# Hybrid block on one core: a weight sum moved ahead in the convolution's projection, stores moved to another engine in the mixing, loads put on another queue at the MLP's seam

## The chip, the core and the metric

The kernel runs on one core of a Trainium2 chip. The metric is device microseconds of one execution; the time of a kernel is the median of its runs. Five engines work side by side, each through its own list of instructions in order: TensorE (PE; its weight loads are shown apart as PEld), VectorE (DVE), ScalarE (ACT), GpSimd (POOL) and SyncE (SP), the last of which only issues transfers here. A transfer is issued by an instruction of one of these engines into a queue and lands some microseconds later. An instruction that needs another's result, or a buffer that is still in use, waits, and everything behind it on its engine waits with it.

## The reference, cut to what matters

```python
SEQ, D_MODEL, CONV_WIDTH, ATTN_WIDTH, D_FF = 512, 2048, 1024, 1024, 8192

h = rmsnorm(x, g_mix)
z = h @ w_in
cb, cc, cv, q, k, v, f_logit, gate_c, gate_a = split(z)
conv_branch = (cb * causal_dwconv(cc * cv, conv_w)) @ w_conv_out
attn_branch = forgetting_attention(q, k, v, log_sigmoid(f_logit + b_f)) @ w_attn_out
merged = sigmoid(gate_c + b_gate_c) * conv_branch + sigmoid(gate_a + b_gate_a) * attn_branch
x = x + merged @ w_mix_out                 # the mixing
h = rmsnorm(x, g_mlp)
u = square(relu(h @ w_ff1))                # first MLP product
x = x + u @ w_ff2                          # second MLP product
return rmsnorm(x, g_final)
```

One batch, one layer, everything in float32.

## The kernel before, in words

All large products are float32 at float32's accuracy, made from a faster format: each operand is split into a high part (`th`, a rounding by ScalarE, line 111) and a low part (`tl`, the rest, a subtraction by VectorE, line 114), and TensorE adds three products: high by high, low by high (lines 171 and 175, or 195 and 197), and high by low (line 177, or 199).

On top of that, each product of two matrices is done by quarters with seven products in place of eight. They are named A11, A12, A22 (quarters as they are) and S1, S2, S3, S4 (sums of quarters). For each of the seven the weights' quarter or sum is made in place by `sub` (VectorE, line 128), split into `th` and `tl`, and multiplied with the matching sum of the activations. The accumulators are `a`, `b`, `c`, `d`; `snap` (ScalarE, line 268, `o<-a`) and `plus` (VectorE, line 131, `o<-c,o`) bring them out and combine them, and `put` takes the finished quarter. A `Group` is one such product for a block of columns: `head` does A11 and A12, and `tail`, `tail2` or `tail3` do the rest in different orders. Its weights are loaded by SyncE into four slots (`x0` to `x3`).

The order of instructions on each engine is set by a scheduler from the program's order, except where `keep_in_program_order` pins an instruction or `issue_after` ties it to another. Four stages matter here.

*Conv.* `conv_out(c, banks)` multiplies the convolution's output by `w_conv_out`, for c = 0 to 3, 512 columns each, with `Columns` groups and `tail2`. The weights' tiles are called `y`, and the stationary operand `ys`. Behind A12 the hook `group.after["A12"]` makes the first sum (`first_sum`, X00 <- X01 - X00, S1's operand). The sum for S3 (X01 <- X11 - X01) is made in `tail2`, behind the call that runs S1. Blocks 0 and 3 multiply their result by gates (`merged<-o,gates`, line 1235, for block 0) that are loaded into four tiles under the tag `hg`.

*Mixing.* Four groups g multiply `merged` by `w_mix_out`. While group g + 1 runs, `Mix` forms the seven operands of group g's result for the MLP. `Mix.out` writes five of them: it splits an operand into `staged` (high, ScalarE) and the operand itself (low, VectorE), and stores both in `h_d` with transfers issued by GpSimd (line 1416). There are fifteen such pairs, since group 3 keeps its parts on chip.

*First MLP product.* `ff1(g, ...)` makes 16 groups of columns of `h @ w_ff1`. The list `later` holds work put off from the group before: applying ReLU and square, forming sums (`r`, `rh`) of the result and storing them to `s_d` (lines 1464 to 1484). `tail` runs that list behind S2's `snap` and ahead of S3.

*Seam.* The second MLP product runs in units, `unit(seg, cg, ST)`, each with four 1 MB weight tiles `y` (line 1708), and with operands `us` that `load_sums` reads back from `s_d` (line 1607): `US[1]` holds those of S2 and S3, `US[2]` of S1 and A22, `US[3]` of S4. For the first unit, `US[1]` is loaded by GpSimd right behind the last group of the first product, and `US[2]` and `US[3]` by SyncE in the middle of the unit's code.

Of the kernel before, what the change touches and what calls it, by code (L numbers as in the profile page):

```python
# [8 lines left out]
F32 = mybir.dt.float32  # L9
# [6 lines left out]
P = 128  # L16
# [29 lines left out]
def tile_hybrid_block(ctx: ExitStack, tc, x, g_mix, w_in, b_f, b_gate, conv_w, w_conv_out,  # L46
# [168 lines left out]
    class Group:  # L215
# [3 lines left out]
        def __init__(self, view, c1, c2, w, ST, mm, banks, put, scale=1.0, extra={}, after=None, shift=SHIFT):  # L219
            self.extra, self.after, self.shift = extra, {} if after is None else after, shift  # L220
            self.view, self.cs, self.w, self.ST, self.mm, self.banks = view, (c1, c2), w, ST, mm, banks
            self.put, self.scale, self.at = put, scale, {}
            self.begun, self.queue, self.X = False, nc.sync, {}
            self.pinned, self.mid, self.apart, self.ready = False, {}, False, {}
            self.freed, self.summed, self.paced, self.half = lambda: None, False, False, {}
            self.nq = view.shape[0] // (2 * P)

        def load(self, i, j):
# [105 lines left out]
        def tail(self):  # L334

            X = self.quarters((0, 1), (1, 1))
            a = self.a
            c = self.acc("c")
            self.run(c, "S4", X[1, 1], True)
            sub(X[0, 0], X[0, 1], X[0, 0])  # L340
            sub(X[0, 1], X[1, 1], X[0, 1])
            sub(X[1, 1], X[1, 1], X[0, 0])
            self.run(a, "S2", X[1, 1], False)
            sub(X[1, 0], X[1, 0], X[1, 1])
            self.done(1, 1)
# [44 lines left out]
        def tail2(self):  # L390

            X = self.quarters((0, 1), (0, 0), (1, 1), (1, 0))
            a = self.a
            if not self.pinned:
                sub(X[0, 0], X[0, 1], X[0, 0])
            c = self.acc("c")
            self.run(c, "S1", X[0, 0], True)
            if not self.summed:
                third = sub(X[0, 1], X[1, 1], X[0, 1])
            if self.pinned and not self.summed:  # L400
                tc.keep_in_program_order(third)
# [744 lines left out]

    class Columns(Group):


        def load(self, i, j):  # L1150
            if (1 - i, j) not in self.at:
                self.at[i, j] = main.tile([P, 2, self.nq, self.w], F32, tag=f"x{slot()}", name=f"y{j}")
            else:
                self.at[i, j] = self.at[1 - i, j]
            t, c = self.at[i, j][:, i], self.cs[j]
# [57 lines left out]
    def conv_out(c, banks):  # L1213

        gates = {}
        if c in GATED:
            for i, j in ((0, 0), (1, 1), (0, 1), (1, 0)):
# [14 lines left out]
        def put(i, j, v):  # L1232
            ts = slice(i * HS, (i + 1) * HS)
            if c == 0:
                nc.vector.tensor_tensor(out=whole_of[c][:, i, :, j, :], in0=v, in1=gates[i, j], op=ALU.mult)
# [121 lines left out]
    class Mix:  # L1357
# [50 lines left out]
        def out(self, n, src):  # L1408
# [3 lines left out]
            else:  # L1412
                hi = staged()
                split_in_order(src, hi, src)
                for e, o in enumerate((hi.bitcast(F32), src)):
                    nc.gpsimd.dma_start(out=h_d[:, SPLIT.index(n), e, 2 * g:2 * g + 2], in_=o)

        def first_of(self):
            self.s1 = pm.tile([P, 2, HS], F32, tag="s1", name="s1")
# [181 lines left out]
    def load_sums(seg, ks, ST, queue=nc.gpsimd):  # L1601

        for k in ks:
            place, names = US[k]
            t = main.tile([P, 2, 4, len(names), HS], F32R, tag=f"t{place}", name="us")
            for e in range(2):
                queue.dma_start(out=t[:, e].bitcast(F32), in_=s_d[seg][:, e, :, 2 * k:2 * k + len(names)])
# [12 lines left out]
    later.pop()()  # L1620
    ph.close()
    pp.close()
# [70 lines left out]
    def unit(seg, cg, ST):  # L1693
# [9 lines left out]
        for i, j in ((0, 1), (1, 1), (0, 0), (1, 0)) if end else ((0, 0), (1, 0), (0, 1), (1, 1)):  # L1703
# [4 lines left out]
            nc.sync.dma_start(out=t, in_=src[i])  # L1708
            X[i, j] = t

        def run(ps, n, src, first):
            hi, lo = parts([P, 4, S])
            split(src, hi, lo)
            mm_rows(ps, ST[n], hi, lo, first)

        last = seg == NSEG - 1
        begun = set()
# [67 lines left out]
        into(1, 0, a)  # L1785
        run(d, "S3", X[0, 1], True)
        free.append(at[0, 1])
        into(1, 1, d)
        run(a, "S1", X[0, 0], False)
# [51 lines left out]
```

## Time and profile before

| | |
|---|---|
| time, median of 3 runs | 2413.63 us (2411.69 to 2413.76) |
| profiled execution | 2415.49 us |
| its span on the engines | 2413.4 us |
| TensorE busy | 2396.1 us (99%), 17778 matmuls |
| VectorE, ScalarE, GpSimd busy | 2029.7, 1205.2, 297.8 us |
| clock granted to TensorE | full speed (tenths of 9 in all 40 slices) |
| transferred | 491.98 MB, mean 204 GB/s |

How to read it: times in the trace are microseconds from the start of the span. A row of the timeline has its start, its duration, the engine, the line of the code, the operation, output and inputs, the shape, and in brackets the idle time ahead of it with what ended it. TensorE's matmuls overlap, so a matmul of 128x256 is listed with 0.28 us, while the next one starts 0.113 us later: gaps are read from start to start. TensorE idles for 17.3 us of the span in all.

### The profile page before, as it was taken

What the parts mean: (1) busy time and instruction counts of PE and PEld (TensorE: products, weight loads), DVE (VectorE), ACT (ScalarE), POOL (GpSimd) and SP (SyncE); (2) the same over time, 40 slices, a digit from 0 to 9 for tenths busy, and PEclk for the clock granted to TensorE, in tenths of its full rate; (3) what the DMA queues carried; (4) which work ended last, traced back from release to release, by engine and by line L of the source; (5) the groups of instructions that cost most, each with busy time, mean ns of one, the idle gap of its engine ahead of it and who ended that gap; (6) DMA issues with size and microseconds to landing.
All of it is one profiled execution on the core that took longest, in us unless ns stands there. A gap on an engine that the chain in (4) does not pass through costs nothing. (4 is left out here: it accounts for less than half of the span.)

```text
span 2413.4 us, 41364 instructions
## 1 busy us (share of the span) xinstructions
PE 2396.1 (99%) x17778; PEld 2259.7 (94%) x17778; DVE 2029.7 (84%) x1683; ACT 1205.2 (50%) x1238; POOL 297.8 (12%) x476
## 2 busy tenths in 40 slices
PE   9999999999999999999999999999999999999998
PEld 9999999999999999899999999999998888888886
DVE  7987677789888778889988889888887888889898
ACT  7443444445555534456666666665664333333334
POOL 1110111121111112023300000000011001100000
PEclk9999999999999999999999999999999999999999
DMA  8664544564565756566856564655678567665662
GB/s 276 190 189 152 156 147 152 154 205 158 172 209 175 262 180 209 165 211 223 311 195 217 194 231 172 222 207 197 231 294 293 165 209 253 218 211 184 233 230 102
DMA packets 281127, 491.98 MB, mean 204 GB/s; under 512 B 11820, under 2 KB 192136, under 8 KB 280560
## 3 DMA queue, kind: packets, MB, share of 16 engines
q1 hardware_dynamic: 228496, 275.86, 36.1%
q0 software_dynamic: 51840, 212.42, 24.0%
q8 instruction: 139, 2.28, 0.4%
q10 hardware_dynamic: 608, 1.06, 0.1%
q14 instruction: 44, 0.36, 0.0%
HBM read 379.70 MB, written 109.07 MB: 203 GB/s over the span
## 5 line engine op out<-in xcount | busy, mean ns | idle before, releaser
L111 ACT ACTIVATE th<-x 128x2048 fp32r<-128x2048 f32 (+1 forms) x280 | 537.1, 1918 | 487.9 <-DVE x L128 165.4
L114 DVE TENSOR_TENSOR tl<-x,th 128x2048 fp32r<-128x2048 f32 (+2 forms) x282 | 639.7, 2274 | 156.2 <-ACT th L111 152.4
L128 DVE TENSOR_TENSOR x<-x,x 128x2048 f32<-128x2048 f32 (+1 forms) x160 | 366.1, 2288 | 22.0 <-DMA x<-in_w_in_dram 16.9
L111 ACT ACTIVATE th<-y 128x2048 fp32r<-128x2048 f32 (+1 forms) x109 | 185.3, 1701 | 272.1 <-PE a L197 138.8
L114 DVE TENSOR_TENSOR tl<-y,th 128x2048 fp32r<-128x2048 f32 (+1 forms) x109 | 219.0, 2014 | 28.3 <-ACT th L111 27.8
L195 PE MATMUL a<-th,us 128*128 128x512 f32 x512 | 199.3, 389 | 0.0
L197 PE MATMUL a<-th,us 128*128 128x512 f32 x512 | 199.2, 389 | 0.0
L171 PE MATMUL c<-S,th 128*128 128x256 f32 x848 | 196.0, 277 | 0.0
L175 PE MATMUL c<-S,th 128*128 128x256 f32 x848 | 195.8, 277 | 0.0
L171 PE MATMUL a<-S,th 128*128 128x256 f32 x784 | 182.4, 278 | 0.2 <-ACT o L268 0.2
L175 PE MATMUL a<-S,th 128*128 128x256 f32 x784 | 180.8, 276 | 0.0
L171 PEld LDWEIGHTS c<-S,th 128*128 128x128 f32 x848 | 159.3, 188 | 0.1
L175 PEld LDWEIGHTS c<-S,th 128*128 128x128 f32 x848 | 159.3, 188 | 0.0
L171 PEld LDWEIGHTS a<-S,th 128*128 128x128 f32 x784 | 147.3, 188 | 0.9 <-issue 0.5
L175 PEld LDWEIGHTS a<-S,th 128*128 128x128 f32 x784 | 147.3, 188 | 0.5 <-issue 0.5
L199 PE MATMUL a<-tl,us 128*128 128x512 f32 x512 | 136.9, 389 | 0.6 <-DVE tl L114 0.6
L171 PE MATMUL b<-A,th 128*128 128x256 f32 x544 | 126.2, 278 | 1.4 <-ACT th L111 1.4
L171 PE MATMUL a<-A,th 128*128 128x256 f32 x544 | 126.8, 279 | 0.0
L171 PE MATMUL d<-S,th 128*128 128x256 f32 x544 | 126.3, 278 | 0.0
L171 PE MATMUL d<-A,th 128*128 128x256 f32 x544 | 125.8, 277 | 0.0
L175 PE MATMUL a<-A,th 128*128 128x256 f32 x544 | 125.7, 277 | 0.0
L175 PE MATMUL b<-A,th 128*128 128x256 f32 x544 | 125.6, 277 | 0.0
(407 smaller groups left out, 6028.4 us busy)
## 6 DMA issues: line engine op xcount, KB each, us to landing
x<-in_w_in_dram SPq DMA_DIRECT2D x86, 1024.0 KB, 6.0
y<-in_w_ff_dram SPq DMA_DIRECT2D x64, 1024.0 KB, 7.7
x<-in_w_ff_dram SPq DMA_DIRECT2D x60, 1024.0 KB, 8.2
us<-s_d POOLq DMA_DIRECT2D x46, 1024.0 KB, 9.5
s_d<-rh POOLq DMA_DIRECT2D x32, 896.0 KB, 5.7
s_d<-r POOLq DMA_DIRECT2D x32, 896.0 KB, 6.1
x<-in_w_mix_out_dram SPq DMA_DIRECT2D x17, 1024.0 KB, 6.8
g_d<-o POOLq DMA_DIRECT2D x32, 256.0 KB, 3.1
```

The source lines that it names most:

```text
L111: return tied(nc.scalar.activation(out=hi, in_=src, func=AF.Copy))
L114: return tied(nc.vector.tensor_tensor(out=lo, in0=src, in1=hi.bitcast(F32), op=ALU.subtract))
L128: return nc.vector.tensor_tensor(out=out, in0=a, in1=b, op=ALU.subtract)
L171: i = nc.tensor.matmul(o, hi[:, q, js], Sh, start=first and q == 0 and j == 0, stop=False, skip_group_check=True)
L175: nc.tensor.matmul(o, hi[:, q, js], Sl, start=False, stop=False, skip_group_check=True)
L195: tied(nc.tensor.matmul(o, Sh, hi[:, q, :], start=begin and q == 0, stop=False, skip_group_check=True))
L197: tied(nc.tensor.matmul(o, Sl, hi[:, q, :], start=False, stop=False, skip_group_check=True))
L199: tied(nc.tensor.matmul(o, Sh, lo[:, q, :], start=False, stop=q == nq - 1, skip_group_check=True))
```

## The change

There are five edits.

1. Conv: `two_sums` makes the sum for S3 right behind the first sum, pinned in that order, after A12; `tail2` leaves it out by the flag `third`. The four gates of a block become one tile, `four`, of one place, and for c = 2 the second weight tile uses that place and not a weight slot. The gated product of block 0's quarter (0, 0) is put on `later`, which `tail2` empties behind S3.
2. Mixing: ScalarE, and not GpSimd, issues the store of the high part in `Mix.out`, pinned in program order.
3. First MLP product, g = 1: with `late` the list `later` is run behind S3 and its `snap`, not ahead of S3.
4. Seam: `US[1]`, `US[2]` and `US[3]` are all loaded on SyncE's queue, right behind the four weight tiles of the first unit.
5. Seam: in the first unit the sum `sub(t2, X10, t2)` for S4 is issued behind the low part of S3.

```diff
+        def two_sums(self):
+            self.first_sum()
+            X = self.quarters((1, 1))
+            tc.keep_in_program_order(sub(X[0, 1], X[1, 1], X[0, 1]))
+            self.third = True
...
# tail
-            while later:
+            while later and not self.late:
                 later.pop(0)()
             d = self.acc("d")
             self.run(d, "S3", X[0, 1], True)
             self.done(0, 1)
             d1 = self.snap(d, self.scale)
+            while later:
+                later.pop(0)()
...
# tail2
-            if not self.summed:
+            if not self.summed and not self.third:
                 third = sub(X[0, 1], X[1, 1], X[0, 1])
...
# Columns.load
+                if self.beside and j == 1:
+                    self.at[i, j] = pc_.tile(shape, F32, tag="hg", name=f"y{j}")
+                else:
+                    self.at[i, j] = main.tile(shape, F32, tag=f"x{slot()}", name=f"y{j}")
...
# conv_out
-                gates[i, j] = pc_.tile([P, 2, HS], F32, tag="hg", name="gates", bufs=4)
+            four = pc_.tile([P, 4, 2, HS], F32, tag="hg", name="gates")
+                gates[i, j] = four[:, n]
...
+                if (i, j) == (0, 0):
+                    later.append(gated)
+                else:
+                    gated()
...
-        group.after["A12"], group.apart = group.first_sum, True
+        group.after["A12"], group.apart, group.beside = group.two_sums, True, c == 2
...
# Mix.out
-                for e, o in enumerate((hi.bitcast(F32), src)):
-                    nc.gpsimd.dma_start(out=h_d[:, SPLIT.index(n), e, 2 * g:2 * g + 2], in_=o)
+                tc.keep_in_program_order(
+                    nc.scalar.dma_start(out=h_d[:, SPLIT.index(n), 0, 2 * g:2 * g + 2], in_=hi.bitcast(F32)))
+                nc.gpsimd.dma_start(out=h_d[:, SPLIT.index(n), 1, 2 * g:2 * g + 2], in_=src)
...
# first MLP product
+        group.late = g == 1
...
-    load_sums(0, (1,), us0)
...
# unit
+        begins = seg == 0 and cg == 0
+        if begins:
+            load_sums(0, (1, 2, 3), us0, nc.sync)
...
-        if seg == 0 and cg == 0:
-            load_sums(0, (2, 3), us0, nc.sync)
...
-        sub(t2, X[1, 0], t2)
+        if not begins:
+            sub(t2, X[1, 0], t2)
+        into(1, 0, a)
+        low = run(d, "S3", X[0, 1], True)
+        if begins:
+            with tc.issue_after(low.ins):
+                sub(t2, X[1, 0], t2)
```

What this does to the order of instructions, at the places that matter. A number behind a name tells buffers apart, and `x2` means two in a row.

VectorE in the conv's block 0, between A12 and S3, before (`y_9254` holds the quarters X00 and X10, `y_9318` X01 and X11; so the first sum is `y_9254<-y_9318,y_9254`, and the sum for S3 `y_9318<-y_9318`):

```order
L114 TENSOR_TENSOR tl<-y_9254,th 128x1024
L128 TENSOR_TENSOR y_9254<-y_9318,y_9254 128x1024
L114 TENSOR_TENSOR tl<-y_9254,th 128x1024
L128 TENSOR_TENSOR y_9318<-y_9318 128x1024
L131 TENSOR_TENSOR o<-b,o 128x512
L128 TENSOR_TENSOR y_9254<-y_9318,y_9254 128x1024
L1235 TENSOR_TENSOR merged<-o,gates 128x2x256
L114 TENSOR_TENSOR tl<-y_9318,th 128x1024
L114 TENSOR_TENSOR tl<-y_9254,th 128x1024
```

And now:

```order
L114 TENSOR_TENSOR tl<-y_9251,th 128x1024
L128 TENSOR_TENSOR y_9251<-y_9315,y_9251 128x1024
L128 TENSOR_TENSOR y_9315<-y_9315 128x1024
L114 TENSOR_TENSOR tl<-y_9251,th 128x1024
L128 TENSOR_TENSOR y_9251<-y_9315,y_9251 128x1024
L131 TENSOR_TENSOR o<-b,o 128x512
L114 TENSOR_TENSOR tl<-y_9315,th 128x1024
L1252 TENSOR_TENSOR merged<-o,gates 128x2x256
```

The sum for S3 stands one `tl` earlier, and the gated product behind a `tl` that it stood ahead of.

ScalarE in the mixing, from the first `staged` of group 0's parts to the `th` of S3 in group 1, before:

```order
L111 ACTIVATE staged<-f 128x512
L111 ACTIVATE th<-x_11421 128x2048
L111 ACTIVATE staged<-f 128x512
L111 ACTIVATE staged<-s_11390 128x512
L268 ACTIVATE o<-d 128x512
L111 ACTIVATE staged<-f 128x512 x2
L111 ACTIVATE th<-x_11309 128x2048
```

And now:

```order
L111 ACTIVATE staged<-f 128x512
L1438 DMA h_d<-staged 128x512
L111 ACTIVATE th<-x_11415 128x2048
L111 ACTIVATE staged<-f 128x512
L269 ACTIVATE o<-d 128x512
L1438 DMA h_d<-staged 128x512
L111 ACTIVATE staged<-s_11384 128x512
L1438 DMA h_d<-staged 128x512
L111 ACTIVATE staged<-f 128x512
L1438 DMA h_d<-staged 128x512
L111 ACTIVATE th<-x_11303 128x2048
```

Four issues stand on ScalarE, and one `staged` of the five has moved behind that `th`. Elsewhere in this stage, in group 3, three matmuls of `c<-th` (S4), which stood ahead of eight `a<-tl`, stand some forty instructions later on TensorE.

ScalarE in the first MLP product, group 1, around S3, before:

```order
L1492 ACTIVATE o<-o,common 128x512
L1469 ACTIVATE r<-c 128x512
L1464 ACTIVATE r<-o 128x256
L1464 ACTIVATE c<-o 128x512
L111 ACTIVATE th<-x_13212 128x2048
L1480 ACTIVATE rh<-r 128x1792
L111 ACTIVATE th<-x_13210 128x2048
L268 ACTIVATE o<-a 128x512
```

And now:

```order
L1515 ACTIVATE o<-o,common 128x512
L1492 ACTIVATE r<-c 128x512
L111 ACTIVATE th<-x_13206 128x2048
L1487 ACTIVATE r<-o 128x256
L1487 ACTIVATE c<-o 128x512
L1503 ACTIVATE rh<-r 128x1792
L111 ACTIVATE th<-x_13204 128x2048
L269 ACTIVATE o<-a 128x512
```

Two operations moved behind the `th` of S3; `rh` and the `th` of S1 still precede `o<-a`.

VectorE in the first unit of the second MLP product, from S2's operand to S1's low part, before:

```order
L114 TENSOR_TENSOR tl<-t_19644,th 128x2048
L1481 TENSOR_TENSOR r<-r,rh 128x1792
L128 TENSOR_TENSOR t_19644<-y_19638,t_19644 128x2048
L114 TENSOR_TENSOR tl<-y_19640,th 128x2048
L114 TENSOR_TENSOR tl<-y_19636,th 128x2048
```

And now:

```order
L114 TENSOR_TENSOR tl<-t_19644,th 128x2048
L1504 TENSOR_TENSOR r<-r,rh 128x1792
L114 TENSOR_TENSOR tl<-y_19631,th 128x2048
L128 TENSOR_TENSOR t_19644<-y_19629,t_19644 128x2048
L114 TENSOR_TENSOR tl<-y_19627,th 128x2048
```

The low part of S3 stands ahead of the sum for S4. On SyncE's queue the `us` loads behind the four weights are six now, four before:

```order
L1733 DMA y_19627<-in_w_ff_dram 128x4x512
L1733 DMA y_19629<-in_w_ff_dram 128x4x512
L1733 DMA y_19631<-in_w_ff_dram 128x4x512
L1733 DMA y_19633<-in_w_ff_dram 128x4x512
L1630 DMA us<-s_d_80 128x4x512 x4
L1630 DMA us<-s_d_80 128x4x256 x2
```

GpSimd's two `us` loads behind the last group are gone.

More of the change, by code (lines that the diff above doesn't have):

```diff
@@ L225, in __init__ @@
             self.freed, self.summed, self.paced, self.half = lambda: None, False, False, {}
+            self.late, self.third = False, False
             self.nq = view.shape[0] // (2 * P)
@@ L397, in tail2 @@
             self.run(c, "S1", X[0, 0], True)
-            if not self.summed:
+            if not self.summed and not self.third:
                 third = sub(X[0, 1], X[1, 1], X[0, 1])
-            if self.pinned and not self.summed:
-                tc.keep_in_program_order(third)
+                if self.pinned:
+                    tc.keep_in_program_order(third)
             d = self.acc("d")
@@ L1147, in tile_hybrid_block @@
     class Columns(Group):
+        beside = False
         def load(self, i, j):
             if (1 - i, j) not in self.at:
-                self.at[i, j] = main.tile([P, 2, self.nq, self.w], F32, tag=f"x{slot()}", name=f"y{j}")
+                shape = [P, 2, self.nq, self.w]
+                if self.beside and j == 1:
+                    self.at[i, j] = pc_.tile(shape, F32, tag="hg", name=f"y{j}")
+                else:
+                    self.at[i, j] = main.tile(shape, F32, tag=f"x{slot()}", name=f"y{j}")
             else:
@@ L1216, in conv_out @@
         if c in GATED:
-            for i, j in ((0, 0), (1, 1), (0, 1), (1, 0)):
-                gates[i, j] = pc_.tile([P, 2, HS], F32, tag="hg", name="gates", bufs=4)
+            four = pc_.tile([P, 4, 2, HS], F32, tag="hg", name="gates")
+            for n, (i, j) in enumerate(((0, 0), (1, 1), (0, 1), (1, 0))):
+                gates[i, j] = four[:, n]
                 k = 4 * c + 2 * j
@@ L1234, in put, with gated @@
             if c == 0:
-                nc.vector.tensor_tensor(out=whole_of[c][:, i, :, j, :], in0=v, in1=gates[i, j], op=ALU.mult)
+                def gated():
+                    nc.vector.tensor_tensor(out=whole_of[c][:, i, :, j, :], in0=v, in1=gates[i, j], op=ALU.mult)
+                if (i, j) == (0, 0):
+                    later.append(gated)
+                else:
+                    gated()
             elif c > 1:
@@ L1606, in load_sums @@
             for e in range(2):
-                queue.dma_start(out=t[:, e].bitcast(F32), in_=s_d[seg][:, e, :, 2 * k:2 * k + len(names)])
+                i = queue.dma_start(out=t[:, e].bitcast(F32), in_=s_d[seg][:, e, :, 2 * k:2 * k + len(names)])
+                if queue is nc.sync:
+                    tc.keep_in_program_order(i)
             for e, n in enumerate(names):
@@ L1709, in unit @@
             X[i, j] = t
+        begins = seg == 0 and cg == 0
+        if begins:
+            load_sums(0, (1, 2, 3), us0, nc.sync)
         def run(ps, n, src, first):
             hi, lo = parts([P, 4, S])
-            split(src, hi, lo)
+            low = split(src, hi, lo)[1]
             mm_rows(ps, ST[n], hi, lo, first)
+            return low
         last = seg == NSEG - 1
@@ L1782, in unit @@
         sub(X[0, 1], X[1, 1], X[0, 1])
-        sub(t2, X[1, 0], t2)
+        if not begins:
[5 more added lines that the diff above has]
+                sub(t2, X[1, 0], t2)
         free.append(at[1, 0])
-        into(1, 0, a)
-        run(d, "S3", X[0, 1], True)
         free.append(at[0, 1])
```

## The prediction

> **What bounds the kernel.** I read the busy shares first, then TensorE's own waits (columns: total us, times, longest us).
>
> ```profile
> PE 2396.1 (99%) x17778; PEld 2259.7 (94%) x17778; DVE 2029.7 (84%) x1683; ACT 1205.2 (50%) x1238; POOL 297.8 (12%) x476
> ...
> PE d L195 <- ACT th L111: 1.1, 1, 1.1
> PE d L199 <- DVE tl L114: 0.8, 2, 0.6
> PE a L199 <- DVE tl L114: 0.6, 1, 0.6
> ```
>
> TensorE is busy for 2396.1 of the span's 2413.4 us, and the change takes no matmul away. So there are two things to win: the 17.3 us in which it stands, and the rate at which it runs. No wait here is much over 1 us. I therefore took the stages that the diff touches one by one: where TensorE stands there, what ends that, and whether the new order removes it. The 2.1 us of the profiled 2415.49 that lie outside the span stay.
>
> **Conv.** Three weight loads wait in this stage; the first of them I follow back.
>
> ```profile
> PEld d L164 <- ACT th L111: 0.4, 1, 0.4
> PEld d L177 <- DVE tl L114: 0.3, 1, 0.3
> PEld c L171 <- DVE o L131: 0.3, 1, 0.3
> ...
> 888.93 1.22 DVE L114 TENSOR_TENSOR tl<-y,th 128x1024 fp32r<-128x1024 f32 x1 [1.19 <-ACT th L111]
> 890.07 1.22 DVE L128 TENSOR_TENSOR y<-y 128x1024 f32<-128x1024 f32 x1
> 891.40 1.06 ACT L111 ACTIVATE th<-y 128x1024 fp32r<-128x1024 f32 x1 [2.51 <-PE c L175]
> 892.52 0.36 PE L164 MATMUL d<-ys,th 128*128 128x192 f32 x1 [0.21 <-ACT th L111]
> ```
>
> The sum `y<-y` of 890.07 makes the operand of S3. It stands behind a `tl` ahead of which VectorE idled 1.19 us, waiting for the `th`. The change puts the 1.22 us sum into this hole: the `tl` comes 0.03 later, the sum more than 1 us earlier. S3's `th` is then bound by the place that TensorE frees (`PE c`, row 891.40). The sum ended at 891.29, just before that `th` began, so I can't tell which of the two was last; the 0.4 goes wholly or not at all, and I take wholly, since the sum is the operand itself. In block 0 the deferred gated product leaves the way of a `tl` and of an `o`, so the two waits of 0.3 go as well. Each stall also slows the first matmul behind it by 0.1 (0.38 against 0.28 in the rows of 1085 and 1088 below). So -0.4 - 0.3 - 0.3 - 0.3 = -1.3, between -0.5 (the first alone) and -1.6. The lent place has a price only if block 3's gates come late: they wait now for block 2's weights to be used up, and are read at block 3's end, so I take 0. The weights of blocks 2 and 3 are issued earlier on the same queue, which can't delay their use.
>
> **Mixing.** Fifteen stores of a high part go from GpSimd to ScalarE. The first rows show where `staged` (the high part's buffer) ran out, the next where three matmuls of S4 moved, and the last an issue by ScalarE elsewhere.
>
> ```profile
> 1074.68 0.58 ACT L268 ACTIVATE o<-d 128x512 f32<-128x512 f32 x1
> 1074.86 1.07 POOL L1416 DMA_DIRECT2D h_d<-staged  x2
> 1081.92 0.63 ACT L111 ACTIVATE staged<-f 128x512 fp32r<-128x512 f32 x1 [6.66 <-DMA h_d<-staged]
> 1083.27 1.90 ACT L111 ACTIVATE th<-x 128x2048 fp32r<-128x2048 f32 x1
> 1085.22 0.38 PE L195 MATMUL d<-th,M 128*128 128x256 f32 x1 [1.14 <-ACT th L111]
> ...
> 1152.23 2.29 DVE L114 TENSOR_TENSOR tl<-x,th 128x2048 fp32r<-128x2048 f32 x1
> 1154.03 0.39 PE L195 MATMUL c<-th,M 128*128 128x256 f32 x1 [1.13 <-ACT o L268]
> ...
> 2397.43 0.37 ACTq L1672 DMA_DIRECT2D out_dram<-x  x1
> ```
>
> ScalarE waited 6.66 us for a store to land, and the `th` of S3 behind it held TensorE for 1.14. In the new order one `staged` less stands ahead of that `th` and one issue more: the `th` starts at 1081.92 + 0.63 + 0.37 = 1082.92, not 1083.27, so 0.35 is gained if the store lands when it did. That it lands earlier no row shows: ScalarE issues it behind the `o<-d` of 1074.68, at about the time GpSimd did (1074.86). With the whole wait gone it is 1.14 + 0.1 and the 0.4 of the `tl` behind that `th`, 1.65. Between 0.35 and 1.65 I take the middle, 1.0, because the nearest row (issue to landing 7 us) belongs to another queue. Against me stands the Trainium skill, "DMA: Bandwidth & Descriptors", section "Issuing engines are not separate DMA queues": a DMA runs on the same 16 engines whichever engine issues it, and only the time of issuing is saved. By it this term would be 0.35.
>
> At 1154.03 TensorE has stood for 1.13 and next needs the `tl` of 1152.23, which ends at 1154.52. Three matmuls on `c` filled 0.35 of that time; they now come behind it and cost 3 x 0.113 (the pace below) = +0.35. Mixing is -0.65, from -1.8 to +0.6 (the 15 issues then delay a `th` by 0.6 more than they free). Those take 15 x 0.37 = 5.6 us of ScalarE, half idle; 15 x 0.53 = 8 us leave GpSimd, 12% busy.
>
> **First MLP product, second group.** Here a stall of 0.38 us does more than stall.
>
> ```profile
> 1239.97 1.71 ACT L1480 ACTIVATE rh<-r 128x1792 fp32r<-128x1792 f32 x1 [2.74 <-issue]
> 1241.58 1.90 ACT L111 ACTIVATE th<-x 128x2048 fp32r<-128x2048 f32 x1
> 1243.38 0.57 ACT L268 ACTIVATE o<-a 128x512 f32<-128x512 f32 x1
> 1244.01 0.38 PE L171 MATMUL a<-S,th 128*128 128x256 f32 x1 [0.22 <-ACT o L268]
> 1244.23 0.28 PE L175 MATMUL a<-S,th 128*128 128x256 f32 x1
> ...
> 1246.94 0.28 PE L171 MATMUL a<-S,th 128*128 128x256 f32 x1
> ...
> 1088.58 0.28 PE L195 MATMUL d<-th,M 128*128 128x256 f32 x1
> ...
> 1090.28 0.28 PE L197 MATMUL d<-th,M 128*128 128x256 f32 x1
> ...
> 1110.24 0.28 PE L197 MATMUL d<-th,M 128*128 128x256 f32 x1
> ...
> 1111.89 0.28 PE L197 MATMUL d<-th,M 128*128 128x256 f32 x1
> ...
> 1210.00:1240.00 30.00, 30.00 (x265) 29.94 (x265) 26.54 (x22) 17.78 (x20) 1.16 (x2) 1.00 0.46 162
> 1250.00:1310.00 60.00, 60.00 (x512) 60.00 (x511) 53.82 (x41) 36.02 (x37) 3.20 (x6) 1.00 0.55 190
> 1320.00:1380.00 60.00, 60.00 (x532) 60.00 (x531) 50.98 (x40) 37.35 (x40) 3.03 (x6) 1.00 0.59 204
> ```
>
> The last three rows are stretches of time: length, then each engine's busy time with its instructions (TensorE first), and the granted clock third from the end. At clock 1.00 throughout, a matmul takes 30/265 = 113.2 ns before the stall, 60/512 = 117.2 behind it, and 60/532 = 112.8 later. The change of pace is at the stall: 1244.23 to 1246.94 holds 23 steps of 117.8 ns. It ends between the last two stretches, where the first matmul of 192 columns stands, so it lasts some 68 us. Twenty matmuls fewer in 60 us are 20 x 0.113 = 2.3 us, 2.6 in 68. So TensorE can come out of a stall in either pace: behind the stall of 1085.22 the 15 steps from 1088.58 to 1090.28 are of 113.3. Of seven stalls ahead of 256-column matmuls in the touched stages, five came out at 113 and two at 118.
>
> The change runs deferred ReLU work (`r`, `c`) behind the `th` of S3 and not ahead of it. `rh` and a `th` still stand ahead of `o<-a`, for which TensorE waits, and `rh` now follows that work: replaying the new order with the durations above, `o<-a` comes 0.1 to 0.2 later, +0.15. But the stall falls otherwise, and its restart is drawn again; five in seven are fast, -2.6. Sum -2.45, from -3.1 (no stall, nor its restart) to +0.6 (a longer one, slow).
>
> **Seam to the second product.** VectorE is late here because transfers are.
>
> ```profile
> 1792.20 2.29 DVE L128 TENSOR_TENSOR y<-y,y 128x2048 f32<-128x2048 f32 x1 [2.13 <-DMA y<-in_w_ff_dram]
> 1804.88 0.39 PE L197 MATMUL a<-th,us 128*128 128x512 f32 x1
> 1805.89 1.21 PE L199 MATMUL a<-tl,us 128*128 128x512 f32 x4 [0.62 <-DVE tl L114]
> 1807.69 2.29 DVE L128 TENSOR_TENSOR t<-y,t 128x2048 f32<-128x2048 f32 x1
> 1808.79 1.07 PE L199 MATMUL a<-tl,us 128*128 128x512 f32 x4
> 1809.89 4.49 DVE L114 TENSOR_TENSOR tl<-y,th 128x2048 fp32r<-128x2048 f32 x2
> 1811.28 0.39 PE L197 MATMUL d<-th,us 128*128 128x512 f32 x1
> 1812.23 1.20 PE L199 MATMUL d<-tl,us 128*128 128x512 f32 x4 [0.56 <-DVE tl L114]
> ```
>
> VectorE waited 2.13 us for a weight `y` while two 1 MB loads of `us` from GpSimd's queue shared the DMA engines with it, and was then busy almost without a gap until 1814. TensorE stands twice: 1805.89 - 1804.88 - 0.23 = 0.78 and 1812.23 - 1811.28 - 0.23 = 0.72, and the restarts cost 0.14 and 0.13 (1.21 and 1.20 against 1.07): 1.77. With `us` behind the weights on one queue VectorE can win up to 2.13, of which the first stall needs 0.8. The second goes by the order alone, since `t<-y,t` (2.29) now comes behind the `tl` of S3. Late next would be the `tl` of S1, second of the 4.49; it keeps its place, and TensorE needs it only after another round of S3. I take -1.75, from -0.85 (weights no earlier) to -2.0.
>
> **Sum.** -1.3 - 0.65 - 2.45 - 1.75 = -6.15, on 2415.49 gives 2409.3. That execution lies 1.86 above the median, 2413.63. Runs of one program can differ by that much through a slow stretch like the one above (2.6) rather than through its waits, so I take it that the median run has already half of the 1.86 of what I hope to win in pace: 2409.3 - 0.93 = 2408.4.
>
> **Rivals.**
> 1. *The waits go, the pace stays.* The second group restarts at 118, as two of seven do: 2408.4 + 2.6 = 2411.0. For it: `o<-a` still comes behind `rh`.
> 2. *The issuer doesn't matter.* Mixing wins 0.35 and loses 0.35: 2408.4 + 0.65 = 2409.05. This is the page's rule named above; for it, the point of issue is the same.
> 3. *More pace is redrawn.* Mixing runs slow in places too (1110.24 to 1111.89 is 14 steps of 117.9), and the change moves work around its transposes. One more stretch of 68 us won: 2408.4 - 2.6 = 2405.8. The like may be lost, which is in the range.
> 4. *Slower.* The `us` of S2 and S3 now queue behind the weights. S2 starts seven steps of 0.23 before 1804.88, at 1803.2, and each us that they land later costs one. To outweigh everything by 0.2% they must land 2418.5 - 2408.4 = 10 us late, at 1813. Against it: the whole seam moves the same bytes as before.
>
> Chances: forecast 0.46, rivals 0.25, 0.11, 0.12, 0.06. A measurement of this kernel can't tell 0.2%, 4.8 us, from no change: faster is below 2408.8. The forecast with its own range, 2406.5 to 2410, lies below it for two thirds, rival 2 for nearly a half, rival 3 wholly, rival 1 for a tenth: 0.31 + 0.05 + 0.12 + 0.02 = 0.50. Slower has rival 4 and a little: 0.07. The range goes down to rival 3 with mixing at its best (-1.15): 2404.6, taken as 2404.5; and up to rival 1 with conv at -0.5 and mixing at +0.25: 2412.7.
>
> **What would show it.** Conv: no wait of `d L164` on `th`. Mixing: ScalarE's 6.66 shorter and TensorE's 1.14 under 0.3. Second group: 530 matmuls in the 60 us from 1250, not 512. Seam: neither `<-DVE tl` in the first unit. I am wrong if stretches at 117 ns turn up where there were none, or if `o<-a` makes a stall of over 0.6.

## The result: 0.2% faster, and the profile after

The changed kernel takes 2409.73 us in the median of 20 runs (2407.84 to 2412.95), the kernel before 2413.93 in 20 runs beside it (2411.51 to 2420.04). The ratio is 0.998, with a 95% interval of 0.9975 to 0.9986: 4.2 us less. The runs also lie closer together, over 5.1 us and not 8.5.

The page of the profiled execution (2409.38 us, span 2407.7) begins like this:

```profile
span 2407.7 us, 41373 instructions
...
PE 2390.4 (99%) x17778; PEld 2255.7 (94%) x17778; DVE 2030.5 (84%) x1683; ACT 1203.8 (50%) x1238; POOL 287.4 (12%) x459
```

TensorE's own waits in it (total us, times, longest):

```profile
PE d L195 <- ACT th L111: 1.0, 1, 1.0
PE ptr L1413 <- DVE o L1396: 1.0, 1, 1.0
PE a L199 <- DVE tl L114: 0.8, 1, 0.8
PE c L171 <- DVE o L131: 0.5, 1, 0.5
PE a L171 <- ACT o L269: 0.4, 1, 0.4
```

TensorE is busy for 5.7 us less, although it does the same 17778 matmuls, and idles for 17.3 us as before. By this page alone the gain would be pace and not waits. But a matmul of 128x256 is listed with 0.28 us and the next one starts 0.113 us later, so up to 0.17 us of each stall counts as busy time: the starts have to decide. Some waits are gone, others are new (`ptr`, `c L171`).

The matmuls stand nearly in the same order in both kernels, so the two traces can be laid on each other: the time from the start of one matmul to the start of another is a stage, and the stages can be compared over all executions profiled here. The table (worked out from the starts of the same four pairs of matmuls, by their places in the trace of before; names are those of the runs below) has us; none of the stages left out differs by more than 0.7 us between any two.

```
edits of the kernel            run              conv      mixing     2nd group  seam
                                                838-1000  1000-1192  1228-1320  1795-1830
none                           before           162.11    192.08     91.95      35.05
late                           e1_late          163.18    190.45     92.21      37.39
none, one matmul more          e2_spare         164.11    193.03     90.69      34.32
none, two matmuls more         e13_two          163.57    192.84     90.07      34.28
seam order                     e6_order         162.53    191.91     90.34      37.58
mixing                         e8_mix           163.53    191.58     90.84      34.43
conv                           e3_conv          160.50    191.50     89.39      34.25
seam loads                     e5_loads         162.37    192.46     89.61      33.12
all                            after            160.50    191.68     89.78      33.09
all but mixing                 e4_nomix         160.50    191.68     92.83      33.09
all, S4 of block 3 later       e7_paced         160.28    190.50     91.94      33.39
all, S4 later, list behind o   e9_behind        160.44    194.24     89.03      33.09
no mixing, list behind o       e12_nomix_behind 160.53    191.59     90.44      33.09
the same, a matmul less        e14_bare         160.50    191.23     88.94      33.09
```

In the pair of before and after the conv gives 1.61, the mixing 0.40, the second group 2.17 and the seam 1.96 us. But read down a column: the conv and the seam stay what they are wherever the edit is in, while the mixing and the second group vary as much without their edit as with it.

### The profile page after: what moved, and what is told of

It is laid out like the page before. It is cut to its first block, busy times and chain, and to the rows that moved or that the text cites. A ratio compares the mean times of both kernels' runs of the same rounds, so it can differ in the third digit from the quotient of the medians.

```text
span 2407.7 us, 41373 instructions
## 1 busy us (share of the span) xinstructions
PE 2390.4 (99%) x17778; PEld 2255.7 (94%) x17778; DVE 2030.5 (84%) x1683; ACT 1203.8 (50%) x1238; POOL 287.4 (12%) x459
## 4 chain that ended last, share of the span: by engine, by line
PE 91%; issue 4%; DVE 2%; ACT 1%; DMA 1%; POOL 1%; SPq 0%; DVEq 0%; POOLq 0%; ACTq 0%
PE a L171 6%; PE a L177 6%; PE a L175 6%; PE a L199 5%; PE a L197 5%; PE a L195 5%; PE d L171 5%; PE d L175 5%; PE d L177 5%; PE c L171 4%; PE c L177 4%; PE c L175 4%; PE d L197 3%; PE d L199 3%; PE d L195 3%
## 5 line engine op out<-in xcount | busy, mean ns | idle before, releaser
L171 PE MATMUL c<-S,th 128*128 128x256 f32 x848 | 195.7, 277 | 0.0
L171 PE MATMUL a<-S,th 128*128 128x256 f32 x784 | 182.0, 278 | 0.4 <-ACT o L269 0.4
L171 PEld LDWEIGHTS c<-S,th 128*128 128x128 f32 x848 | 159.3, 188 | 0.0
L171 PEld LDWEIGHTS a<-S,th 128*128 128x128 f32 x784 | 147.2, 188 | 1.1 <-ACT o L269 0.6
L199 PE MATMUL a<-tl,us 128*128 128x512 f32 x512 | 136.8, 389 | 0.0
L171 PE MATMUL b<-A,th 128*128 128x256 f32 x544 | 126.0, 277 | 1.4 <-ACT th L111 1.4
L171 PE MATMUL a<-A,th 128*128 128x256 f32 x544 | 126.5, 278 | 0.0
L171 PE MATMUL d<-S,th 128*128 128x256 f32 x544 | 126.2, 278 | 0.0
L171 PE MATMUL d<-A,th 128*128 128x256 f32 x544 | 125.6, 277 | 0.0
L175 PE MATMUL d<-S,th 128*128 128x256 f32 x544 | 125.4, 276 | 0.0
```

The costliest lines, as they stand in the source:

```text
L171: i = nc.tensor.matmul(o, hi[:, q, js], Sh, start=first and q == 0 and j == 0, stop=False, skip_group_check=True)
L175: nc.tensor.matmul(o, hi[:, q, js], Sl, start=False, stop=False, skip_group_check=True)
L199: tied(nc.tensor.matmul(o, Sh, lo[:, q, :], start=False, stop=q == nq - 1, skip_group_check=True))
```

## The experiments

Each is a kernel with one part of the change, or with one part undone, timed in five rounds (e13_two in three) against the kernel before on the same chip.

**The second group's edit alone** (before with `group.late = g == 1` and the two loops over `later`).

> The kernel before with edit 3 alone (the deferred list of the first MLP product's second group run behind S3). Theory (the stall is not shortened, its restart is redrawn and comes out fast): TensorE's stall ahead of S1's matmuls on a is 0.5 to 0.65 us, not 0.38; behind it 256-column matmuls step at 113 ns, 528 to 532 of them in the 60 us from 1250; time 2.2 us below the kernel before. Rival (pace belongs to the place in the program and not to how the stall ended): 512 matmuls in that stretch, time within 0.5 us of the kernel before. Second rival (the pace is drawn anew in every execution): a time about 1 us below, with a spread as wide as before's.

2415.87 us against 2414.73, ratio 1.0006 (0.9997 to 1.0015): no gain. The stretch from 1250 in this kernel and, for comparison, in the changed one (time, then each engine's busy time with its instructions, TensorE first; the clock is third from the end):

```profile
1250.00:1310.00 60.00, 60.00 (x512) 60.00 (x511) 53.85 (x41) 36.02 (x38) 3.19 (x6) 1.00 0.53 187
```

```profile
1250.00:1310.00 60.00, 60.00 (x532) 60.00 (x531) 55.35 (x42) 38.09 (x39) 3.19 (x6) 1.00 0.51 182
```

With the edit alone the stall is 0.65 us (a gap of 0.76 between starts, less 0.11), as the theory had it, but TensorE came out of it at the slow pace. In the changed kernel it came out at the fast one.

**One matmul of 192 columns more behind the stall.**

```diff
+        if g == 1:
+            group.extra = {**apart(0, "S2", 0), **apart(0, "S1", 1)}
```

> The kernel before with one matmul more, of 192 columns, as fifth behind the stall of 1244 in the second group of the first MLP product (S1); its result is used by nobody; nothing else is changed. Theory (the slow pace starts with the stall and lasts until a matmul of another width): the stall stays at 0.38 us, the 256-column matmuls behind the added one step at 113 ns, about 530 in the 60 us from 1250 and not 512; time 2.6 - 0.1 = 2.5 us below the kernel before. Rival (what is slow there is the work itself, or its operands' places): still about 117 ns and no gain, 0.1 us slower.

2413.90 us, ratio 1.0001 (0.9992 to 1.0009). The added matmul, at 1247.5, didn't end the slow pace; the group's next one, at 1275.4, did, 37 us earlier than in before:

```profile
1250.00:1310.00 60.00, 60.00 (x523) 60.00 (x522) 52.48 (x40) 36.04 (x37) 3.19 (x6) 1.00 0.56 194
```

523 lies between 512 and 530: neither theory holds as it was written. The slow pace can be ended, so it isn't the work itself, but one matmul of another width ends it only sometimes.

**The mixing's edit undone** (the changed kernel with both stores on GpSimd).

> The changed kernel with edit 2 undone (both stores of the mixing issued by GpSimd again). Theory (who issues the store doesn't matter, and the later fifth store costs a transpose 1 us): the wait of 1.0 us of the transposes near 1096 is gone, the stall ahead of S3's matmuls on d near 1084 is 1.4 us and not 1.3, the stage from 960 to 1195 is within 1 us of the changed kernel's, and so is the time. Rival (ScalarE's issue is worth the 0.65 us of the prediction or more): the stage is longer by 0.7 us or more.

2409.96 us, against 2409.73 of the changed kernel: no difference that these runs can tell. The stage takes 191.68 us in both. The wait at the transposes goes as expected, 0.3 us here and not 1.0; the one ahead of S3's `d` is 1.2 us here, against 1.0 in the changed kernel. This execution, with `late` in, ran slow from 1231 to 1311, the longest such stretch of all: 92.83 in the table.

**S4 of the conv's block 3 behind `o<-c,o`.**

```diff
         group.after["A12"], group.apart, group.beside = group.two_sums, True, c == 2
+        group.paced = c == 3
```

The stall it aims at is new with the change. On VectorE a `tl` stands ahead of `o<-c,o`, which frees TensorE's accumulator:

```profile
934.63 1.22 DVE L114 TENSOR_TENSOR tl<-y,th 128x1024 fp32r<-128x1024 f32 x1
935.76 0.68 DVE L131 TENSOR_TENSOR o<-c,o 128x512 f32<-128x512 f32 x1
...
936.50 0.38 PE L171 MATMUL c<-ys,th 128*128 128x256 f32 x1 [0.47 <-DVE o L131]
```

> The changed kernel, and in the conv's block 3 the operand of S4 is split behind the sum o<-c,o, on which TensorE's accumulator c waits. Theory (the stall of 0.63 us ahead of S4's matmuls near 936.5, new with the change, comes from VectorE's order): the stall goes, the conv is 0.7 us shorter, time 0.7 us below the changed kernel, some 2409. Rival (TensorE then waits for the later tl of S4 instead): the stall moves to c<-ys,tl and the gain is under 0.3 us.

2409.09 us, ratio 0.9975 (0.9966 to 0.9984). The stall is gone and 838 to 945 is 105.15 us and not 105.85, but the 55 us behind it take 0.48 longer (55.13 against 54.65): 0.2 us remain. What takes the time there wasn't followed up.

**Conv alone** (edit 1 on the kernel before).

> The kernel before with edit 1 alone (conv). Theory (the stages' waits add up): the three stalls of the conv go, the new one of 0.6 us ahead of S4's matmuls in block 3 comes, together 1.5 us less from 840 to 945; time 1.5 us below the kernel before, with a spread over its runs as wide as the kernel before's (about 8 us), since the seam is as it was. Rival (the conv is worth nothing beyond what one execution showed): within 0.5 us of the kernel before.

2412.65 against 2415.01 us, ratio 0.9989 (0.9980 to 0.9997), about 2.4 us by the medians. Its spread was 4.3 us in 11 runs and not as wide as before's, 9.8 in 29. The five executions with the edit and block 3 as the change has it agree within 0.03 us from 838 to 1000; the seven without it range over 2.0. The theory's 1.5 was too little and its spread wrong. One reason shows in an execution without the edit (e2_spare):

```profile
848.91 1.22 DVE L128 TENSOR_TENSOR y<-y,y 128x1024 f32<-128x1024 f32 x1
851.11 0.69 DVE L1235 TENSOR_TENSOR merged<-o,gates 128x512 f32<-128x512 f32 x1 [0.97 <-DMA gates<-g_d]
851.72 2.35 DVE L114 TENSOR_TENSOR tl<-y,th 128x1024 fp32r<-128x1024 f32 x2
```

The gated product waits 0.97 us for the gates to land, the `tl` behind it waits with it, and TensorE's gap at 853 is 1.24 us, where the execution of the prediction had 0.39. Putting that product behind the `tl` takes most of a wait away that the profile before hardly showed (in e9_behind, with the edit, it still waits 0.63 us for the gates, and that part of the block is 0.26 longer).

**Seam: the loads alone, and the order alone** (edits 4 and 5 on the kernel before).

> The kernel before with edit 4 alone (the us loads on SyncE's queue behind the weights). Theory (the wait of VectorE for a weight tile at the seam is the changeable part of it and differs between executions): both stalls of the first unit go, 1.7 us or more, time 2 to 3 us below the kernel before, and the spread over the runs narrows from 8 us to about 5. Rival (the order of VectorE is needed too): the stall ahead of S3's low part stays at 0.5 us or more, time 1 us below.

> The kernel before with edit 5 alone (the sum for S4 behind S3's low part at the seam). Theory: S3's stall of 0.72 us goes, S2's of 0.78 stays or varies, 0.85 us less at the seam, time 0.5 to 1 us below the kernel before, spread as wide as before's. Rival (the loads alone matter): the seam is as long as before, no change.

The loads alone: 2411.66 us against 2415.01, ratio 0.9987 (0.9979 to 0.9996), over 4.7 us in 11 runs; TensorE has no wait from 1795 to 1835, the stage is 33.12 us. The order alone: 2413.79, ratio 0.9995 (0.9987 to 1.0004), no gain shown in the time. In its execution the weight landed later still, and a stall came in A12's low part (`b`), which the order can't help; VectorE's rows first, then TensorE's waits:

```profile
1794.50 2.29 DVE L128 TENSOR_TENSOR y<-y,y 128x2048 f32<-128x2048 f32 x1 [5.58 <-DMA y<-in_w_ff_dram]
...
1809.99 2.28 DVE L114 TENSOR_TENSOR tl<-y,th 128x2048 fp32r<-128x2048 f32 x1
1812.19 2.28 DVE L128 TENSOR_TENSOR t<-y,t 128x2048 f32<-128x2048 f32 x1
```

```profile
PE b L199 <- DVE tl L114: 2.0, 1, 2.0
PE a L199 <- DVE tl L114: 0.3, 1, 0.3
```

S3's wait (`d L199`) is missing here, as the theory had it, late as the weight is. All six executions without either edit of the seam have it, 0.72 to 0.76 us by the starts; these are the waits of e1_late, where the weight was 4.50 us late:

```profile
PE a L195 <- ACT th L111: 1.0, 1, 1.0
PE b L199 <- DVE tl L114: 0.9, 1, 0.9
PE a L199 <- DVE tl L114: 0.6, 1, 0.6
PE d L199 <- DVE tl L114: 0.6, 1, 0.6
```

The stage of e6_order is long all the same, 37.58 us, because of the stall in `b` and of what came behind it: seven steps of 0.43 us between matmuls of 512 columns, and not 0.23, at a granted clock of 0.50 (third from the end), some 1.5 us:

```profile
1801.40:1804.40 3.00, 3.00 (x8) 2.31 (x7) 3.00 (x3) 0.92 (x1) 0.00 (x0) 0.50 0.85 275
```

The instruction that waits for the weight, in the changed kernel, and S2's and S3's low parts behind it:

```profile
1786.42 2.29 DVE L128 TENSOR_TENSOR y<-y,y 128x2048 f32<-128x2048 f32 x1 [0.20 <-DMA y<-in_w_ff_dram]
...
1797.77 2.29 DVE L114 TENSOR_TENSOR tl<-t,th 128x2048 fp32r<-128x2048 f32 x1
...
1801.91 2.29 DVE L114 TENSOR_TENSOR tl<-y,th 128x2048 fp32r<-128x2048 f32 x1
```

The wait for that weight is 1.2 to 5.6 us in the seven executions without the loads' edit (2.13 in before), and 0 to 1.4 in the seven with it. In e5_loads VectorE didn't wait for it at all, so this execution shows the stalls gone without the order, and not that the order is never needed. Two others bear on that: with the weight 1.36 us late and neither edit (e3_conv) TensorE waits ahead of S3's low part, with it 1.41 us late and both edits (e7_paced) it doesn't, and the stage is 34.25 and 33.39 us. This is TensorE's wait in e3_conv, and VectorE's in e7_paced, where TensorE has none in the stage:

```profile
PE d L199 <- DVE tl L114: 0.6, 1, 0.6
```

```profile
1788.11 2.29 DVE L128 TENSOR_TENSOR y<-y,y 128x2048 f32<-128x2048 f32 x1 [1.41 <-DMA y<-in_w_ff_dram]
```

**The deferred list behind `o<-a`** (with the conv's correction).

```diff
             s2 = self.snap(a)
+            taken = self.snapped if self.late else None
...
             while later:
-                later.pop(0)()
+                with tc.issue_after(taken.ins):
+                    later.pop(0)()
```

> The changed kernel with S4's operand in the conv's block 3 behind o<-c,o (as in the run that did this alone), and in the first MLP product's second group the deferred list, rh with it, behind the snap o<-a on ScalarE and VectorE. Theory (the stall ahead of S1's matmuls comes from rh and brings the slow pace with it, almost always here): no stall there, no slow stretch from 1240 to 1308, 530 matmuls in 60 us of it; 2.6 us less than with the conv's correction alone, 2406.5. Rival (the pace turns slow anyhow, at a matmul of 192 columns or another stall nearby): the stall's 0.4 us alone are gained, 2408.7.

2408.71 us in 6 runs, ratio 0.9969 (0.9957 to 0.9981). No stall ahead of S1 and no slow stretch in the group: 89.03 us. Of the theory's 2.6 us only 0.4 are seen in the medians (2409.09 to 2408.71), and 1.4 in the ratios (0.9975 to 0.9969); six runs can't tell these apart. That the conv's correction alone doesn't always run slow there would explain it, but isn't shown. The execution profiled had the longest mixing of all (194.24), with 2.0 us ahead of `a<-tl`, behind which 15 matmuls stepped at 0.213 us at a granted clock of 0.50 (1.5 us more), and 1.6 at the transposes:

```profile
PE a L199 <- DVE tl L114: 2.0, 1, 2.0
PE ptr L1416 <- DVE o L1399: 1.6, 1, 1.6
```

**The mixing's edit alone** (edit 2 on the kernel before).

> The kernel before with edit 2 alone (the high part's stores issued by ScalarE). Theory (the wait is for the landing, whoever issues; the fifth pair's later store gives back what one staged less wins): the mixing from 1000 to 1192, 190.5 to 193.0 us in the executions without the edit, lies in the same band; the time is within 1 us of the kernel before. Rival (the prediction's 0.65 us or more): 191.2 us or less, time 0.7 to 1.8 us below.

2413.94 against 2415.18 us, ratio 0.9998 (0.9989 to 1.0007), which leaves room for the 0.65; 191.58 us in the mixing, inside the band. The stall ahead of S3's `d` is away here, and 1.6 us stand at the transposes.

**No mixing edit, list behind `o<-a`.**

> The changed kernel with edit 2 undone and the deferred list of the second group behind the snap o<-a (conv's block 3 as in the changed kernel). Theory (conv 2.2, seam 2.2 and the pace of the second group 1.5 to 2.5 us add up, and the mixing's edit is worth nothing): the stretch from 1228 to 1320 takes 89.0 to 89.1 us, the time is 2408 to 2409, 1 us below the changed kernel. Rival (the mixing's edit was worth something after all): over 2409.7.

2408.24 us (2406.87 to 2409.55, 8 runs), ratio 0.9971 (0.9960 to 0.9981). The time is as expected, the stretch isn't: 90.44. A gap of 0.20 between starts, 0.09 of it a stall, at the group's own 192-column matmul at 1230.6 was enough to turn the pace, until the next one at 1270.4:

```profile
1240.00:1270.00 30.00, 30.00 (x257) 30.00 (x256) 26.64 (x21) 19.49 (x19) 2.13 (x4) 1.00 0.57 208
1275.00:1305.00 30.00, 30.00 (x267) 30.00 (x266) 24.42 (x18) 17.58 (x18) 2.13 (x4) 1.00 0.63 214
```

**Two matmuls of 192 columns more**, as in e2_spare, at rows 1 and 2.

> The kernel before with two matmuls more of 192 columns behind the stall of the second group, four ordinary ones apart, where one did not end the slow pace. Theory (a slow stretch of 118 ns is ended by the second matmul of 192 columns behind its start, as at 1312 in the kernel before and at 1275 with one more): 118 ns only up to the second added one if the stall comes out slow, 530 matmuls in the 60 us from 1250. Rival (what ends it is the place in the program, at the next group's own added matmul near 1275 or 1312): slow until there, 512 to 523 matmuls. If the stall comes out fast, it tells nothing.

2414.40 us, ratio 0.9997 (0.9988 to 1.0006). TensorE came out of the stall at the fast pace in the execution profiled (532 matmuls in the 60 us), so it tells nothing of what ends a slow stretch; 2414.40 shows no gain either.

**And one such matmul less**, the group's own.

```diff
-                     extra={"A12": "first", "S3": "first"} if g == 0 else apart(0, "S2", 0))
+                     extra={"A12": "first", "S3": "first"} if g == 0 else {} if g == 1 else apart(0, "S2", 0))
```

> The changed kernel with edit 2 undone, the deferred list of the second group behind o<-a, and without the one matmul of 192 columns whose result nobody uses in that group (near 1231). Theory (a 192-column matmul can start the slow pace as well as end it, as it did at 1231 in two executions; with neither it nor a stall there nothing changes the pace): 113 ns from 1195 to the next one at 1270, 1228 to 1320 in 88.9 to 89.0 us, time 2407.5 to 2408.3, spread under 3 us. Rival (without it the group runs slow from some other cause, for which it was put there): 117 to 118 ns over some of 1195 to 1270, 90.4 us or more, time 2409 or more.

2408.25 us (2406.42 to 2410.86, 10 runs), ratio 0.9975 (0.9965 to 0.9984). The group ran at 113 ns throughout, 88.94 us, as the theory has it:

```profile
1230.00:1260.00 30.00, 30.00 (x266) 30.00 (x266) 26.30 (x22) 21.66 (x24) 1.06 (x2) 1.00 0.59 203
1250.00:1310.00 60.00, 60.00 (x531) 60.00 (x531) 55.34 (x41) 38.53 (x41) 3.19 (x6) 1.00 0.48 172
```

But the theory's condition wasn't met: ahead of S2, near 1229.6, two starts still lie 0.195 us apart, 0.08 of it a stall. Of the thirteen executions that have the matmul there, eleven also went on at 113 ns, so one execution doesn't tell what leaving it out does. The spread was 4.4 us and not under 3, so other stages vary as well. The medians of e7_paced, e9_behind, e12_nomix_behind and e14_bare lie 0.6 to 1.5 us below the changed kernel's, but their intervals overlap its own: none is shown to be faster.

## Why the prediction was right, and where it wasn't

The time lies in the range, 1.3 us above the forecast, and the sign is right. Against the one execution the terms even look exact: 1.3 forecast and 1.61 measured, 0.65 and 0.40, 2.45 and 2.17, 1.75 and 1.96. Against the executions in the table two of the four don't stand, and a third has another size: that the number came out so near is luck in part.

**Conv: right mechanism, half the size.** Without the edit 838 to 1000 takes 163.06 us in the mean of seven executions, with it 160.51 in five: 2.55, not 1.3. Cut at the starts of the same matmuls, the three waits that the prediction named give 1.25 in the execution that it read, as forecast, and 1.6 in the mean, because the gates' landing makes the first of block 0's two up to 0.85 longer. Smaller stalls between 893 and 936, which it didn't count, give 1.1 more; the new stall in block 3, which it didn't see, takes 0.8 back; and the products behind the conv (`pt`, 942 to 960) are 0.6 shorter, which it didn't look at. That the lent place costs nothing holds: no execution waits for block 3's gates.

**Mixing: the term of -0.65 doesn't show.** With the edit the stage takes 192.00 us in the mean of four, without it 191.88 in ten; single ones lie 3.8 us apart, so the mean can't rule out 0.65, but its two parts can be seen. The step that failed is "one `staged` less stands ahead of that `th`", taken as a gain without a cost. The gain is there: the wait ahead of S3's `d` is 1.0, 0, 0 and 0 us in the four executions with the edit, against 0.5 to 3.4 without (1.6 in the mean). But the `staged` left out now stands ahead of the next `th`, and the time is given back:

```profile
1072.44 0.61 ACT L111 ACTIVATE staged<-f 128x512 fp32r<-128x512 f32 x1
...
1073.08 0.33 ACTq L1438 DMA_DIRECT2D h_d<-staged  x1
...
1080.91 0.63 ACT L111 ACTIVATE staged<-f 128x512 fp32r<-128x512 f32 x1 [6.76 <-DMA h_d<-staged]
1081.57 0.33 ACTq L1438 DMA_DIRECT2D h_d<-staged  x1
...
1084.67 0.84 ACT L1422 ACTIVATE f<-ptr,cols 128x256 f32<-128x256 f32 x2 [0.81 <-DMA h_d<-f]
1085.39 0.63 ACT L111 ACTIVATE staged<-f 128x512 fp32r<-128x512 f32 x1
...
1086.48 1.92 ACT L111 ACTIVATE th<-x 128x2048 fp32r<-128x2048 f32 x1
...
1088.43 2.29 DVE L114 TENSOR_TENSOR tl<-x,th 128x2048 fp32r<-128x2048 f32 x1 [0.32 <-ACT th L111]
...
1094.60 0.84 ACT L1422 ACTIVATE f<-ptr,cols 128x256 f32<-128x256 f32 x2 [2.97 <-DMA h_d<-f]
...
1097.59 0.66 PE L1413 MATMUL ptr<-ident,o 128*128 128x128 f32 x4 [0.98 <-DVE o L1396]
```

The fifth `staged` at 1085.39 delays that `th` to 1086.48, VectorE's `tl` and the `o<-o,xr` behind it are late, and the transposes wait 0.98 us. The store of its low part (`h_d<-f`) also comes later and ScalarE waits 2.97 for it. All four executions with the edit have the transposes' wait, 1.0 to 1.6 us, against 0.3 at most without. So neither sign of the prediction came in the profile after: ScalarE's wait for the store is 6.76 us and not shorter than 6.66, and TensorE's 1.0 is not under 0.3. On the store's flight rival 2 was right: from issue to landing it takes 6.3 to 7.7 us with ScalarE's issue, and 6.3 to 7.4 with GpSimd's. By the Trainium skill, "DMA: Bandwidth & Descriptors", section "Issuing engines are not separate DMA queues", only the time of issuing is saved; these durations agree with that. On the point of issue the prediction was wrong: ScalarE doesn't issue the store behind `o<-d` but 0.03 us behind the `staged` (1073.08), GpSimd 0.6 to 1.0 us behind it. With that ScalarE's wait is 5.3 to 5.4 us in the other three executions with the edit, and 6.0 to 6.8 in the ten without. The 0.35 for the three moved matmuls can't be told from the scatter; the wait that they left is 0.8 to 2.0 us with the edit (1.1 in the mean), and 0.3 to 1.3 without (0.8).

**Second group: the term of -2.45 was luck on both sides.** The step that failed is "its restart is drawn again; five in seven are fast". Drawn again it is, but in every execution and in both kernels: behind the stall ahead of S1 six of ten executions went on at the slow pace and four at the fast one, with the edit (e1_late, e7_paced slow, after fast) as without it (before, e2_spare, e6_order, e8_mix slow, e3_conv, e5_loads, e13_two fast); e4_nomix was slow already. The profile before happened to be slow and the one after fast, so the pair shows 2.17 us that the edit doesn't give: alone it is at 1.0006. The prediction took 0.93 off for this; all of the 2.6 belonged off. The stall grew in the pair as forecast, from 0.38 to 0.55 (a gap of 0.66), but it is 0.18 to 0.77 us in the seven executions without the edit and 0.15 to 0.80 in the four with it, so the growth isn't shown to be the edit's. Nor did the slow stretch of the profile before end at its first matmul of 192 columns, as the prediction read it: one stood at 1272.38, and the steps were 117.8 ns from there on to the next at 1312.07.

**Seam: right.** Six executions without the loads' edit take 34.95 us in the mean (34.25 to 37.39; e6_order, with the order, 37.58), seven with it 33.13: 1.8, for 1.75 forecast. That the second stall "goes by the order alone" is borne out by e6_order, and by e7_paced against e3_conv; where the weight comes in time the loads alone end both. The late `us` of rival 4 didn't come.

**The sum.** 2.55 and 1.8 from the table are 4.35, and 4.2 was measured. Two terms of 3.1 us fell, the conv made up for 1.3 of them, and 0.9 had been taken off beforehand: so the forecast is near. Timed alone, the conv and the loads give 2.4 and 3.4 us by the medians, more than the 4.2 of all edits together; as each ratio's interval is some 4 us wide, that is no contradiction.

## What to carry to other kernels

Before a term is taken from a row, ask whether the row would be there in the next execution: a wait behind a transfer, or a pace that a stall set, is one draw, and two profiles that differ by it look like a proof. Laying the same stage of many executions side by side, with each edit alone, showed at once which 1 to 2 us were the edits' and which were not, where the medians could barely. An edit that takes an instruction out of a waiting chain moves it into another: look for the next chain that it joins. And the two edits that paid here took a variable transfer out of the way of the weights' low parts.

## What the runs showed of the hardware

At a granted clock of 1.00, 256-column matmuls run at 113 or at 118 ns, and each of the slow stretches seen in this group lasted 28 to 80 us. Each began at a stall, of as little as 0.09 us, and ended at a matmul of 192 columns: at the first one behind its start in three of eight, at the second in the other five. In two of the eight the stall stood ahead of a matmul of 192 columns, so either may have set the pace. What decides is open; e14_bare, without that matmul and with a stall of 0.08 us there, shows only that this group can do without it. The Trainium skill, "TensorE: Matmul & The Clock Gate", section "Back-to-back issue gap", gives one spacing for a width (N/2.4 + 2.5 ns for a matmul by itself, 109 ns for 256 columns by my estimate); that one width has two lasting ones is what these rows show, and the measurement decides.

Three stalls of 2.1 to 2.9 us (e2_spare near 1088, e6_order near 1800, e9_behind near 1153) were followed, 0.8 to 1.3 us after they ended, by some 3 us at a granted clock of 0.50, which cost about 1.5 us each. No such stretch was seen behind stalls of 2.0 us and less, nor behind the longest, 3.5 us in e13_two; why not is open.
